# An fp32 encoder layer on one core: the down-projection as seven products of half blocks, and the weights' sums spread over four stages

## The chip, the cores and the metric

The kernel runs on one core of a Trainium2 chip. A core has TensorE for matmuls (PE in the profile, its weight loads PEld), VectorE (DVE), ScalarE (ACT), GpSimd (POOL) and SyncE (SP), which in this kernel issues every data transfer. The engines run side by side, each works off its own instructions in order, and semaphores join them. The metric is the device time of one execution in microseconds (us); less is better.

## The reference

One layer on two sequences of 512 tokens, width D = 1024, hidden width 2816, all in fp32. Cut to what matters:

```
mix = sigmoid(gla) * (oa @ w_o_a) + sigmoid(glb) * (ob @ w_o_b)   # "branches"
x = x + gt1 * (mix @ w_out)                                       # output projection
h2 = _rmsnorm(x, g_ffn) * (1 + sc2) + sh2
u = _dwconv(h2 @ w_up, conv_w, conv_b)                            # up-projection, 3-tap convolution over tokens
ua, ug = jnp.split(u, 2, axis=-1)
x = x + gt2 * ((jax.nn.silu(ug) * ua) @ w_down)                   # down-projection
```

Ahead of it stand the norm, the input projections and two kinds of attention (windowed, and over all keys with low-rank projections), which give oa and ob.

## The kernel before, in words

An fp32 operand is split into a high and a low part (`split_fast`: ACT casts, DVE subtracts; `split_pool`: both on POOL), and a product is three matmuls (`mm3`: high·high, high·low, low·high). A matmul takes 128 rows of the one operand against 512 columns of the other.

The stages follow each other on PE, with these starts in the profiled execution: input projections (0), attention with the gates' matmuls between (about 217 us), branches (600.6), output projection (693.4), up-projection (786), down-projection (1217.6).

**Up-projection.** It already is a scheme of seven products on half blocks, for each of 22 chunks of hidden columns: 84 matmuls a chunk instead of 96. It needs sums of the blocks of `w_up`. These are made ahead, during the attention, by the generator `weight_sums`: for each half of a chunk (128x4x256) it loads `wsum` (512 KB), does four POOL operations on it and stores it to `su_d` in DRAM. There are 44 halves, two buffers, and the attention's loop calls `next(wsum, None)` once a unit, three to a half. These instructions are pinned to program order (`keep_in_program_order`), and POOL also does the softmax's scaling (`p`, L539), for which PE's transposes (`ppt`, L545) wait.

**Branches.** `w_branch` loads a piece of w_o and splits it on POOL (`wo`, L70 and L73).

**Output projection.** `project_half(hf, order, between)` makes half the columns for all eight tiles of 128 tokens: 24 matmuls on `psx` a tile, a read-out on DVE, a store to `x1_d` (the trace writes `x_d`, since it leaves numbers out of names). `w_half(hf)` brings the weights in eight pieces through the ring `wraw` (seven buffers) and the ring `wt` (eight). So the eighth piece of `w_half(1)`, needed by the first tile of `project_half(1)`, is loaded only when the first piece has been split, and that waits for the last tile of `project_half(0)`.

**Down-projection.** `down_step(b, k)` brings and splits one block of gated values (`g_d`, stored by the up-projection) and two of `w_down`; for each sequence 22 blocks k, 4 row tiles, 2 column halves and 3 matmuls: 1056 matmuls on `psd`, both sequences one after the other on eight PSUM banks.

The order of the instructions on each engine is laid down when the kernel is built: a scheduler places them, within the rings of buffers and the pinned orders. SP too is in order, and an issue that waits for a semaphore holds all behind it.

Of the kernel before, what the change touches and what calls it, by code (L numbers as in the profile page):

```python
# [8 lines left out]
F32 = mybir.dt.float32  # L9
# [7 lines left out]
D = 1024  # L17
NB = 2
S = 512
TOK = NB * S  # L20
NT = S // 128
# [12 lines left out]
NP = FF // 128  # L34
EPS = 1e-6
# [4 lines left out]
def encoder_block(ctx, tc, x, c_t, w_ada0, b_col, w_ada, b_ada, cols, w_z, w_g, gains, tabs, sink,  # L40
# [11 lines left out]
    g_d = dram.tile([NB, NP, 128, S], F32, name="g_d")  # L52
# [403 lines left out]

    mp = ctx.enter_context(tc.tile_pool(name="mp", bufs=1))
# [5 lines left out]
    with ExitStack() as st:  # L463
# [37 lines left out]

        def weight_sums():

            pin = tc.keep_in_program_order
            halves = [(c, slice(256 * q, 256 * (q + 1))) for c in range(NP) for q in range(2)]
            ts = {}

            def load(n):  # L510
                if n < len(halves):
                    c, cs = halves[n]
                    ts[n] = gw.tile([128, 4, 256], F32, name="wsum", bufs=2)
                    pin(SY.dma_start(ts[n], w_up[c].rearrange("m q p n -> p (m q) n")[:, :, cs]))

            load(0)
            yield
            yield
            for n, (c, cs) in enumerate(halves):
                t = ts[n]  # L520
                load(n + 1)
                pin(G.tensor_add(t[:, 3], t[:, 2], t[:, 3]))
                pin(G.tensor_sub(t[:, 2], t[:, 0], t[:, 2]))
                yield
                pin(G.tensor_sub(t[:, 0], t[:, 3], t[:, 0]))
                pin(G.tensor_sub(t[:, 1], t[:, 1], t[:, 0]))
                yield
                pin(SY.dma_start(su_d[c, :, :, cs], t))
                yield
# [185 lines left out]
        wsum = weight_sums()  # L715
# [11 lines left out]
        for n in range(len(todo) + LAG + 2):  # L727
# [21 lines left out]
            next(wsum, None)  # L749
# [36 lines left out]
    with ExitStack() as s0:  # L786
# [33 lines left out]

        for f in range(0, KD, 2):
            wo = [w_branch(f), w_branch(f + 1)]
            for b in range(NB):
                for q in range(2):
                    branches(f + q, b, wo[q])
            if f == 4:
                ws = w_half(0)
# [7 lines left out]
    DOWN = ("st", "pt", "pt", "h", "h", "h", "h", "st")  # L835
    down = []

    def down_step(b, k):
        tag = DOWN[len(down) % 8]
        blk = hblk("wd", [128, 8 * S]) if tag == "h" else mblk("wd", tag, [128, 8 * S])  # L840
        w = blk[:, 0:4 * S].rearrange("p (a n) -> p a n", a=2)
        g = blk[:, 4 * S:6 * S].rearrange("p (a n) -> p a n", a=2)
        down.append((w, g))
        split_fast(g[:, 0], g[:, 1], wraw(g_d[b, k]))
        for hf in range(2):
            cs = slice(hf * 512, (hf + 1) * 512)
            (split_pool if hf else split_fast)(w[:, 0, cs], w[:, 1, cs], wraw(w_down[k * 128:(k + 1) * 128, cs]))
# [5 lines left out]
    with ExitStack() as s0:  # L853
# [94 lines left out]
        project_half(0, (0, 1), lambda b, i: None)  # L948
# [49 lines left out]
        def gated(c, b, ua, ug):  # L998
            A.activation(ug, ug, AF.Silu)
            V.tensor_mul(ua, ua, ug)  # L1000
            SY.dma_start(g_d[b, c], ua)
# [15 lines left out]
        def rest(c, w, px, val0, between=()):  # L1017
            between = iter(between)
            product(px, next(w), "t2", True)
            u2 = copied(px)  # L1020
            next(between, lambda: None)()
# [5 lines left out]
            next(between, lambda: None)()  # L1027
# [3 lines left out]
            V.tensor_add(u2, u2, py)  # L1031
            product(px, next(w), "t4", True)
            gated(c, 0, ua, conv1(c, 1, px))
            gated(c, 1, conv1(c, 0, u2), conv1(c, 1, p5))

        EARLY, HALVES = 4, 2
        wf = [list(weights_first(c)) for c in range(HALVES)]
# [10 lines left out]
        for c in range(HALVES, EARLY):  # L1048
            started.append(first(weights_first(c)))
            differences(c, c + 1)  # L1050

        for c in range(NP):
            if c < EARLY:
                rest(c, weights_rest(c), *started[c])
            else:
                w = weights_all(c)
                if c == NP - 1:
                    rest(c, w, *first(w), [lambda k=k: down_step(0, k) for k in (1, 2)])
                else:
                    rest(c, w, *first(w))  # L1060
                if c == NP - 2:
                    down_step(0, 0)


    with ExitStack() as s0:
        wk = s0.enter_context(tc.tile_pool(name="wke", bufs=2))
        LATE = 3
        for b in range(NB):
            gt = wk.tile([128, D], F32, name="gtf")
            SY.dma_start(gt, gt_d[1, b].partition_broadcast(128))  # L1070
            pss = [[bank("psd") for _ in range(2)] for _ in range(NT)]

            def products(i, k0, k1, halves=(0, 1)):
                for k in range(k0, k1):
                    w, g = down[b * NP + k]
                    for hf in halves:
                        cs = slice(hf * 512, (hf + 1) * 512)
                        sl = slice(i * 128, (i + 1) * 128)
                        mm3(pss[i][hf], g[:, 0, sl], g[:, 1, sl], w[:, 0, cs], w[:, 1, cs], k == 0, k == NP - 1)

            for k in range(NP):
                if len(down) == b * NP + k:
                    down_step(b, k)
# [85 lines left out]
```

## Time and profile before

| | |
|---|---|
| three runs | 1458.72, 1460.76 and 1462.15 us, median 1460.76 us |
| the profiled execution | 1463.69 us, its span in the trace 1461.9 us |
| granted TensorE clock, mean | 0.989 |
| PE busy | 95% of the span |
| DVE, ACT, POOL busy | 64%, 46%, 42% |

The span runs from the first to the last instruction of the trace. The shares are averages over stages with different limits. A granted clock of 1.00 is TensorE's full speed (2.4 GHz), 0.50 the lower level (1.2 GHz).

### The profile page before, as it was taken

To read this page: it belongs to the slowest core of one execution; us is meant where nothing else is said; L and a number is where in the kernel's file an instruction comes from. 1 tells how busy PE (TensorE), PEld (TensorE's weight loads), DVE (VectorE), ACT (ScalarE), POOL (GpSimd) and SP (SyncE) were. 2 spreads that over 40 slices of the span, in tenths; PEclk is the share of its full clock that TensorE was granted. 3 is DMA by queue.
4 is the path that set the end of the run, shared out by engine and by line. 5 is a ranking of instruction groups with operands and counts; after the bars stand their busy time and mean duration, and the time that the engine had idled before them with its cause. 6 is when DMAs were issued, how large, how long until landed. Compare 5 with 4: busy or idle time off the path is not lost.

```text
span 1461.9 us, 21179 instructions
## 1 busy us (share of the span) xinstructions
PE 1395.4 (95%) x7184; PEld 1155.7 (79%) x7184; DVE 941.7 (64%) x1885; ACT 679.5 (46%) x1385; POOL 609.0 (42%) x702
## 2 busy tenths in 40 slices
PE   5888997999999899999998999999999999999998
PEld 4777776888878787787887888888888887888887
DVE  4788774666668786564369776666666668347433
ACT  3475223666666566332136765555555554212210
POOL 3175023676677787455003232222222235444430
PEclk9999999999999999999999999999999999999999
DMA  8565764666666667855432344444434447646522
GB/s 320 195 209 178 239 234 159 196 227 202 227 198 220 208 212 250 286 174 177 143 115 80 108 130 130 125 127 123 130 123 127 132 122 250 205 140 222 185 80 72
DMA packets 162620, 255.19 MB, mean 175 GB/s; under 512 B 21192, under 2 KB 86984, under 8 KB 159440
## 3 DMA queue, kind: packets, MB, share of 16 engines
q1 hardware_dynamic: 162512, 253.84, 53.2%
q8 instruction: 57, 0.93, 0.3%
q14 instruction: 51, 0.42, 0.1%
HBM read 186.67 MB, written 67.13 MB: 174 GB/s over the span
## 4 chain that ended last, share of the span: by engine, by line
PE 78%; DVE 10%; DMA 5%; POOL 3%; ACT 2%; issue 2%; SPq 0%; ACTq 0%; POOLq 0%; DVEq 0%
PE px L980 15%; PE psg L495 9%; PE py L980 8%; PE psd L80 5%; PE psd L81 5%; PE psd L82 5%; PE pz L980 4%; PE ppt L545 3%; PE ppo L608 2%; PE psx L82 2%; PE psx L81 2%; PE psx L80 2%; PE psz L80 1%; PE psz L82 1%; PE psz L81 1%
## 5 line engine op out<-in xcount | busy, mean ns | idle before, releaser
L959 POOL TENSOR_TENSOR wt<-wraw,wt 128x512 fp32r<-128x512 f32 x88 | 119.4, 1363 | 395.4 <-ACT wt L958 362.9
L980 PE MATMUL px<-t,wt 128*128 128x512 f32 x792 | 190.0, 389 | 1.7 <-ACT tmp_cc L985 1.7
L980 PEld LDWEIGHTS px<-t,wt 128*128 128x128 f32 x792 | 148.5, 188 | 33.1 <-ACT tmp_cc L985 2.4
L495 PE MATMUL psg<-h_hi,wg 128*128 128x512 f32 x512 | 172.1, 401 | 0.0
L77 DVE TENSOR_TENSOR wd<-wraw,wd 128x512 fp32r<-128x512 f32 x88 | 96.3, 1133 | 90.8 <-ACT wd L76 90.8
L80 PE MATMUL psd<-wd 128*128 128x512 f32 x352 | 137.0, 389 | 0.1
L82 PE MATMUL psd<-wd 128*128 128x512 f32 x352 | 136.9, 389 | 0.0
L81 PE MATMUL psd<-wd 128*128 128x512 f32 x352 | 136.9, 389 | 0.0
L76 ACT CAST wd<-wraw 128x512 fp32r<-128x512 f32 x88 | 50.8, 619 | 151.5 <-issue 112.7
L958 ACT CAST wt<-wraw 128x512 fp32r<-128x512 f32 x154 | 93.9, 619 | 39.7 <-POOL wt L959 26.5
L495 PEld LDWEIGHTS psg<-h_hi,wg 128*128 128x128 f32 x512 | 97.0, 192 | 18.7 <-POOL wg L73 0.8
L539 POOL TENSOR_SCALAR p<-p,l 128x512 f32<-128x512 f32 (+2 forms) x128 | 78.3, 615 | 63.7 <-DVE l L538 45.9
L495 PE MATMUL psg<-h_lo,wg 128*128 128x512 f32 x256 | 102.7, 401 | 0.0
L537 ACT ACTIVATE p<-pps,nm 128x512 f32<-128x512 f32 (+2 forms) x128 | 78.1, 610 | 39.2 <-DVE nm L534 31.3
L992 DVE SCALAR_TENSOR_TENSOR tmp_u<-tmp_cc,cw,tmp_u 128x511 f32<-128x511 f32 x66 | 57.2, 867 | 41.5 <-ACT tmp_u L991 41.4
L70 POOL TENSOR_SCALAR wd<-wraw 128x512 fp32r<-128x512 f32 x44 | 33.6, 764 | 112.5 <-PE psd L82 84.9
L80 PEld LDWEIGHTS psd<-wd 128*128 128x128 f32 x352 | 66.1, 188 | 14.3 <-issue 0.5
L82 PEld LDWEIGHTS psd<-wd 128*128 128x128 f32 x352 | 66.1, 188 | 13.8
L81 PEld LDWEIGHTS psd<-wd 128*128 128x128 f32 x352 | 66.1, 188 | 13.5
L534 DVE TENSOR_REDUCE nm<-pps 128x1 f32<-128x512 f32 (+2 forms) x128 | 74.7, 584 | 3.2 <-PE pps L82 1.5
L545 PE MATMUL ppt<-ident,p 128*128 128x128 f32 x416 | 66.9, 274 | 8.2 <-POOL p L539 8.2
L73 POOL TENSOR_TENSOR wd<-wraw,wd 128x512 fp32r<-128x512 f32 x44 | 73.1, 1661 | 3.7
(256 smaller groups left out, 3425.7 us busy)
## 6 DMA issues: line engine op xcount, KB each, us to landing
w_ada<-in_w_ada_dram SPq DMA_DIRECT2D x24, 1024.0 KB, 5.5
wsum<-in_w_up_dram SPq DMA_DIRECT2D x44, 512.0 KB, 3.9
su_d<-wsum SPq DMA_DIRECT2D x44, 512.0 KB, 3.6
wraw<-su_d SPq DMA_DIRECT2D x88, 256.0 KB, 3.1
wraw<-in_w_down_dram SPq DMA_DIRECT2D x88, 256.0 KB, 3.2
wraw<-in_w_up_dram SPq DMA_DIRECT2D x66, 256.0 KB, 2.7
g_d<-tmp_u SPq DMA_DIRECT2D x44, 256.0 KB, 2.4
wraw<-g_d SPq DMA_DIRECT2D x44, 256.0 KB, 3.5
```

Of the source, the lines that this page charges most:

```text
L77: V.tensor_sub(lo, raw, hi.bitcast(F32))
L80: PE.matmul(ps, lhsT=lh, rhs=rh, start=first, stop=False)
L81: PE.matmul(ps, lhsT=lh, rhs=rl, start=False, stop=False)
L82: PE.matmul(ps, lhsT=ll, rhs=rh, start=False, stop=last)
L495: PE.matmul(ps, lhsT=ws[n][:, wl, k, :], rhs=hl[b][:, k, :], start=k == 0 and i == 0, stop=k == KD - 1 and i == 2)
L534: V.tensor_reduce(nm, ps[:, :n], op=ALU.max, axis=AX.X, negate=True)
L537: A.activation(p[:, :n], ps[:, :n], AF.Exp, bias=nm, accum_out=l)
L539: G.tensor_scalar(out=p[:, :plen], in0=p[:, :plen], scalar1=l, scalar2=1.0, op0=ALU.mult, op1=ALU.mult)
L545: PE.transpose(pt[:, j * 128:(j + 1) * 128], p[:, j * 128:(j + 1) * 128], ident)
L958: A.copy(w[:, 0], raw)
L959: lo_eng.tensor_sub(w[:, 1], raw, w[:, 0].bitcast(F32))
L980: PE.matmul(ps[:, sl], lhsT=w[:, wl, i], rhs=h[:, hl, sl], start=not add and i == 0 and n == 0, stop=i == 3 and n == 2, skip_group_check=add)
```

## The change

It has four parts.

1. **The sums of w_up in three places.** `weight_sums(tile, width, count)` now works through the chunks in the order `ORDER` (j, then j+11), of which the up-projection now also takes its chunks: 27 halves in the attention (a `next` at each of the first 62 units, then at every third), 6 halves in the branches (on `wt` tiles, three `next` after each branch), and the rest as 22 quarters of 128 columns in `project_half(0)` (on `cc` tiles, nine `next` after each tile).
2. **The down-projection as seven products.** With A the gated values (two sequences by two halves of the hidden width) and B the blocks of w_down, `PAIRS` names the seven products. Each has 11 steps j, 4 row tiles and 3 matmuls, 924 in all. `down_step()` brings one block of each operand (256 KB each), ACT casts both, DVE subtracts for the left one and DVE or POOL by turns for the right one. Four banks are one product's set, and there are two sets; later products add onto the banks of earlier ones.
3. **The sums for it in the up-projection.** `gated` writes to eight slots `gs`; `left_sums` (four POOL operations and four stores a pair of chunks) and `right_sums` (44 quarters of w_down: two loads, four POOL operations of 128x128, one store to `t_d`) are called from `between`, four times a chunk, right_sums twice a call in the chunks 5 to 20.
4. **Read-outs spread.** After each product four banks are read (one ACT copy or one DVE operation each), and the rest (a product with the gate, an addition of x, the store) goes to a list `later`, of which two entries are done a step, on POOL.

```diff
-        def weight_sums():
-            halves = [(c, slice(256 * q, 256 * (q + 1))) for c in range(NP) for q in range(2)]
+    quarters = [(c, 128 * q) for c in ORDER for q in range(4)]
+    def weight_sums(tile, width, count):
+        pin = tc.keep_in_program_order
+        def load(n):
+            if n < count and quarters:
+                c, c0 = quarters[0]
+                del quarters[:width // 128]
+                t, cs = tile(), slice(c0, c0 + width)
+                pin(SY.dma_start(t, w_up[c].rearrange("m q p n -> p (m q) n")[:, :, cs]))
+                return t, su_d[c, :, :, cs]
+        nxt, n = load(0), 0
+        yield
+        yield
+        while nxt:
+            n += 1
+            (t, dst), nxt = nxt, load(n)
+            pin(G.tensor_add(t[:, 3], t[:, 2], t[:, 3]))
+            pin(G.tensor_sub(t[:, 2], t[:, 0], t[:, 2]))
+            yield
+            pin(G.tensor_sub(t[:, 0], t[:, 3], t[:, 0]))
+            pin(G.tensor_sub(t[:, 1], t[:, 1], t[:, 0]))
+            yield
+            pin(SY.dma_start(dst, t))
+            yield
...
-            next(wsum, None)
+            if n < 62 or n % 3 == 2:
+                next(wsum, None)
...
-        project_half(0, (0, 1), lambda b, i: None)
+        wsum = weight_sums(lambda: tmp("cc").rearrange("p (m n) -> p m n", m=4), 128, 4 * NP)
+        def sums(b, i):
+            for _ in range(9):
+                next(wsum, None)
+        project_half(0, (0, 1), sums)
+        for _ in wsum:
+            pass
         ws = w_half(1)
...
+            def between():
+                next(lsum, None)
+                if n > EARLY and not last:
+                    for _ in range(2):
+                        next(rsum, None)
+                if last:
+                    down_step()
```

SP in the output projection before, from the second store of the first sequence on (`wraw_8304` is the eighth piece of `w_half(1)`):

```order
L885 DMA x1_d_65<-x1_0_8006 128x512
L954 DMA cw_8818<-in_conv_dram 128x176
L885 DMA x1_d_65<-x1_0_8006 128x512 x2
L901 DMA tmp_u0_8309<-gt_d_66 128x512
L885 DMA x1_d_65<-x1_0_8006 128x512
L885 DMA x1_d_65<-x1_1_8007 128x512 x3
L764 DMA wraw_8304<-in_w_out_dram 128x512
L764 DMA wraw_8820<-in_w_up_dram 128x512
```

SP at the same place now: how the quarters begin, and (behind the dots) what stands around the eighth piece, `wraw_8382`:

```order
L914 DMA x1_d_66<-x1_0_7930 128x512
L476 DMA tmp_cc_7967<-in_w_up_dram 128x4x128
L476 DMA tmp_cc_7969<-in_w_up_dram 128x4x128
L991 DMA cw_8896<-in_conv_dram 128x176
L491 DMA su_d_68<-tmp_cc_7967 512x1x128
L476 DMA tmp_cc_7976<-in_w_up_dram 128x4x128
L491 DMA su_d_68<-tmp_cc_7969 512x1x128
...
L491 DMA su_d_68<-tmp_cc_8190 512x1x128
L476 DMA tmp_cc_8236<-in_w_up_dram 128x4x128
L773 DMA wraw_8382<-in_w_out_dram 128x512
L773 DMA wraw_8898<-in_w_up_dram 128x512
```

The eighth piece stood behind stores of x1 alone; now it stands behind the stores of the first 15 quarters (`tmp_cc_8190` is the fifteenth), each with the load of the quarter after next behind it.

POOL in the last third of the attention before (scaling for the transposes, and the sums):

```order
L522 TENSOR_TENSOR wsum_5594<-wsum_5594 128x256
L523 TENSOR_TENSOR wsum_5594<-wsum_5594 128x256
L539 TENSOR_SCALAR p_5704<-p_5704,l_5705 128x384
L525 TENSOR_TENSOR wsum_5594<-wsum_5594 128x256
L526 TENSOR_TENSOR wsum_5594<-wsum_5594 128x256
L539 TENSOR_SCALAR p_5729<-p_5729,l_5730 128x384
L539 TENSOR_SCALAR p_5754<-p_5754,l_5755 128x256
L522 TENSOR_TENSOR wsum_5693<-wsum_5693 128x256
```

POOL in the same third now (L547 is the scaling):

```order
L547 TENSOR_SCALAR p_6068<-p_6068,l_6069 128x384
L547 TENSOR_SCALAR p_6094<-p_6094,l_6095 128x256
L547 TENSOR_SCALAR p_6131<-p_6131,l_6132 128x256
L547 TENSOR_SCALAR p_6154<-p_6154,l_6155 128x384
L547 TENSOR_SCALAR p_6177<-p_6177,l_6178 128x384
L485 TENSOR_TENSOR wsum_5949<-wsum_5949 128x256
L486 TENSOR_TENSOR wsum_5949<-wsum_5949 128x256
L547 TENSOR_SCALAR p_6205<-p_6205,l_6206 128x256
```

Between two halves of sums there now stand about nine scalings instead of three.

POOL in the middle of the up-projection before had the splits of one kind and nothing else:

```order
L959 TENSOR_TENSOR wt_9546<-wraw_9544,wt_9546 128x512
L959 TENSOR_TENSOR wt_9581<-wraw_9579,wt_9581 128x512
L959 TENSOR_TENSOR wt_9586<-wraw_9584,wt_9586 128x512
L959 TENSOR_TENSOR wt_9682<-wraw_9680,wt_9682 128x512
L959 TENSOR_TENSOR wt_9701<-wraw_9699,wt_9701 128x512
```

POOL there now (L1048 is `left_sums`, L1070 to L1073 `right_sums`, L996 the split that was L959):

```order
L996 TENSOR_TENSOR wt_10216<-wraw_10214,wt_10216 128x512
L1048 TENSOR_TENSOR gs_9193<-gs_9193 128x512 x4
L1070 TENSOR_TENSOR tmp_sf_9997<-tmp_sf_9997 128x128
L1071 TENSOR_TENSOR tmp_sf_9997<-tmp_sf_9997 128x128
L1072 TENSOR_TENSOR tmp_sf_9997<-tmp_sf_9997 128x128
L1073 TENSOR_TENSOR tmp_sf_9997<-tmp_sf_9997 128x128
...
L1070 TENSOR_TENSOR tmp_sf_10125<-tmp_sf_10125 128x128
L996 TENSOR_TENSOR wt_10328<-wraw_10326,wt_10328 128x512
```

The splits for the products now queue behind the sums on POOL. (At the dots stands a further quarter of the same form.)

## Rows read from the trace of the kernel before

**Rows 1.** The page, busy time of each engine in the whole span.

```profile
PE 1395.4 (95%) x7184; PEld 1155.7 (79%) x7184; DVE 941.7 (64%) x1885; ACT 679.5 (46%) x1385; POOL 609.0 (42%) x702
```

**Rows 2.** Windows: stretch, its length, busy time and count of each engine, clock, DMA.

```profile
900.00:1000.00 100.00, 100.00 (x443) 82.83 (x442) 63.22 (x84) 55.03 (x90) 26.15 (x20) 1.00 0.43 126
1300.00:1400.00 100.00, 100.00 (x443) 82.84 (x442) 54.88 (x54) 21.58 (x38) 46.36 (x38) 1.00 0.56 186
```

**Rows 3.** The tile psd on PE: ns min/median/max, first and last start.

```profile
L80 PE MATMUL psd<-wd x352: 389/389/468, 1217.6 to 1456.7; 128*128 128x512 f32 x176
```

**Rows 4.** Waits by pair, 250 to 620 us: total, times, longest.

```profile
POOL wsum L522 <- DMA wsum<-in_w_up_dram: 30.0, 14, 4.8
PE ppt L545 <- POOL p L539: 8.2, 5, 3.4
```

**Rows 5.** Timeline of POOL and of PE, 493 to 499 us.

```profile
495.73 0.72 POOL L522 TENSOR_TENSOR wsum<-wsum 128x256 f32<-128x256 f32 x1 [4.84 <-DMA wsum<-in_w_up_dram]
497.23 1.60 POOL L539 TENSOR_SCALAR p<-p,l 128x256 f32<-128x256 f32 x3
497.76 0.44 PE L545 MATMUL ppt<-ident,p 128*128 128x128 f32 x2 [3.36 <-POOL p L539]
```

**Rows 6.** Windows around the stalls of the attention.

```profile
480.00:520.00 40.00, 35.28 (x193) 29.51 (x191) 29.04 (x88) 23.19 (x61) 30.49 (x45) 0.96 0.70 222
580.00:600.00 20.00, 16.45 (x69) 13.26 (x67) 8.29 (x11) 3.92 (x9) 14.02 (x17) 0.91 0.70 225
```

**Rows 7.** Waits of PE by pair, 600 to 800 us.

```profile
PE psy L82 <- POOL wo L73: 2.8, 3, 1.5
PE psy L80 <- POOL wo L70: 1.5, 2, 0.8
```

**Rows 8.** The tile psx on PE, then timelines of DVE and SP, 693 to 740 us.

```profile
L80 PE MATMUL psx<-wt,m_hi x128: 389/389/500, 693.4 to 785.4; 128*128 128x512 f32 x128
705.08 0.69 DVE L884 TENSOR_TENSOR x<-tmp_u,x 128x512 f32<-128x512 f32 x1
705.80 0.33 SPq L885 DMA_DIRECT2D x_d<-x  x1
733.78 0.33 SPq L764 DMA_DIRECT2D wraw<-in_w_out_dram  x1
739.09 0.68 DVE L77 TENSOR_TENSOR wt<-wraw,wt 128x512 fp32r<-128x512 f32 x1
```

**Rows 9.** SP's waits 430 to 610 us, then its timeline at 486 us.

```profile
SPq L528 <- POOL wsum L526: 33.2, 13, 4.4
486.28 0.52 SPq L528 DMA_DIRECT2D su_d<-wsum  x1
```

**Rows 10.** Tiles wsum and wt on POOL; landing of wsum (512 KB); issues of wraw.

```profile
L522 POOL TENSOR_TENSOR wsum<-wsum x44: 722/734/1124, 251.6 to 591.4; 128x256 f32<-128x256 f32 x44
L959 POOL TENSOR_TENSOR wt<-wraw,wt x88: 1263/1296/2850, 786.6 to 1199.0; 128x512 fp32r<-128x512 f32 x88
DMA to landing us min/median/max: 3.2/3.7/8.2
wraw<-su_d SPq DMA_DIRECT2D x88, 256.0 KB, 3.1
wraw<-in_w_up_dram SPq DMA_DIRECT2D x66, 256.0 KB, 2.7
```

**Rows 11.** PE after its idle time at 219 us, and the window behind it.

```profile
223.94 1.11 PE L159 MATMUL psa<-ident,br 128*128 128x128 f32 x4 [5.00 <-DVE br L156]
224.00:230.00 6.00, 6.00 (x19) 4.91 (x20) 2.06 (x13) 0.00 (x0) 0.85 (x3) 0.59 0.33 115
```

**Rows 12.** Groups by form, 1218 to 1462 us: busy, mean ns, idle before.

```profile
L77 DVE TENSOR_TENSOR wd<-wraw,wd 128x512 fp32r<-128x512 f32 x77 | 86.6, 1163 | 90.2 <-ACT wd L76 90.2
L73 POOL TENSOR_TENSOR wd<-wraw,wd 128x512 fp32r<-128x512 f32 x39 | 65.4, 1677 | 3.3
L76 ACT CAST wd<-wraw 128x512 fp32r<-128x512 f32 x75 | 43.1, 619 | 148.1 <-issue 112.7 <-PE psd L82 21.1 <-DMA wraw<-in_w_down_dram 12.3
```

More of the change, by code (lines that the diff above doesn't have):

```diff
@@ L1055, in encoder_block @@
             else:
                 w = weights_all(c)
[L1057 to L1062, printed above, removed]
+                rest(c, w, *first(w), between)
+            if c >= HP:
+                for _ in lsum:
+                    pass
+                lsum = left_sums(c - HP)
+        for _ in lsum:
+            pass
@@ L1065, in encoder_block @@
+        for _ in rsum:
+            pass
     with ExitStack() as s0:
[L1066 to L1067 removed]
+        wk = s0.enter_context(tc.tile_pool(name="wke", bufs=1))
+        AHEAD, LATE = 4, 3
+        gts = []
         for b in range(NB):
[L1069 removed]
+            gt = wk.tile([128, D], F32, name=f"gtf{b}")
             SY.dma_start(gt, gt_d[1, b].partition_broadcast(128))
[L1071 to L1083, printed above, removed]
[L1084 to L1101 removed]
@@ new lines, in encoder_block, with x1_tile, store @@
+            gts.append(gt)
+        sets = [[bank("psd") for _ in range(NT)] for _ in range(2)]
+        q1 = mblk("q1", "st", [128, NT, S], F32)
+        vw = mblk("vw", "st", [128, 2, NT, S], F32)
+        later = []
+        def x1_tile(b, i, n):
+            xt = wk.tile([128, 512], F32, name="xe", bufs=6)
+            t = b * NT + i
+            SY.dma_start(xt, x1_d[t * 128:(t + 1) * 128, n * 512:(n + 1) * 512])
+            return xt
+        def store(b, i, n, src):
+            t = b * NT + i
+            SY.dma_start(out[t * 128:(t + 1) * 128, n * 512:(n + 1) * 512], src)
@@ new lines, in c21, with tile_product @@
+        def c21(i, ps, xt):
+            y = ytile()
+            for h in range(2):
+                cs = slice(h * 256, (h + 1) * 256)
+                V.tensor_mul(y[:, cs], ps[:, cs], gts[1][:, cs])
+                V.tensor_add(y[:, cs], y[:, cs], q1[:, i, cs])
+                t = NT + i
+                SY.dma_start(out[t * 128:(t + 1) * 128, cs], y[:, cs])
+        def tile_product(ps, i, n, first, last, add):
+            sl = slice(i * 128, (i + 1) * 128)
+            g, w, _ = down[n]
+            for m, (gi, wi) in enumerate(((0, 0), (0, 1), (1, 0))):
+                PE.matmul(ps, lhsT=g[:, gi, sl], rhs=w[:, wi], start=first and not add and m == 0,
+                          stop=last and m == 2, skip_group_check=add)
```

191 lines of the change are left out of this document (128 added, 63 removed).

## The prediction

> **What bounds the kernel now.** I read the page's shares first: PE is busy 95% of the span, no other engine above 64% [rows 1]. A share says nothing of the stages, so I looked at windows next. In the up- and the down-projection PE is busy 100 us of 100 at full clock, with 443 matmuls in each stretch, so one costs 100 / 443 = 0.226 us [rows 2]. (The 389 ns that the tile's view gives for one are pipelined and overlap; the pace is what counts.) The 1056 matmuls of psd stand between 1217.6 and about 1457.2 us: 0.227 each, with no gap [rows 3]. There, time falls only with the number of matmuls, and any engine that comes late adds its lateness in full.
>
> Then the waits of PE. In the attention, transposes wait 8.2 us in 5 times for POOL's scaling, while POOL waits 30.0 us for loads of wsum [rows 4]. The timeline shows one such stall whole: POOL sits 4.84 us for a load of wsum, does two sums of the half, comes to the scaling at 497.23, and PE, which needs that, starts after 3.36 us idle [rows 5]. After the stalls the granted clock is below 1.00: 0.96 over 40 us and 0.91 over 20 us [rows 6], which is 40 x 0.04 + 20 x 0.09 = 3.4 us lost. The branches lose 4.3 us to POOL's splits of wo in two groups of waits [rows 7]. The output projection has no PE idle time of note, but little slack, as shown below.
>
> **The change, part by part.** All terms are against the profiled execution's 1463.7 us, which is 2.9 above the median of the runs; I take this off at the end.
>
> *Seven products.* 1056 - 924 = 132 matmuls less, at 0.2265 us: **-29.9**. They are of the same shape, so this holds as long as PE stays the bound.
>
> *Sums in the attention.* The last third of the units keeps a third of the sums; their loads are issued some six scalings ahead of their use, so the waits of rows 4 should go, and the lost clock with them: 8.2 + 3.4 = 11.6. The sums in the first 62 units stay, and a few small stalls may appear elsewhere, for which I take off 1.1: **-10.5** (bounds: -11.6, all of it; -5, if the two long stalls of some 3.4 us come back elsewhere).
>
> *Sums in the branches.* 6 halves x 4 operations x 0.74 us = 18 us more of POOL in the first seven branches, each 24 matmuls = 5.4 us of PE. The wait there is already for POOL, but wo is split a pair of pieces ahead, and the 6 halves spread: **+0.5** (-1 to +3, where the upper end lets a third of the 18 us minus the idle time of POOL come through).
>
> *Quarters in the output projection.* This is the term that I take as the main loss. Call T0 = 693.4, the first psx [rows 8]. The order of SP shows two facts. The first quarter's load stands behind the first store of x1, and that was issued at 705.80, after DVE's 705.08 operation [rows 8]: T0 + 12.4. And the eighth piece of w_out's second half stands behind the store of the fifteenth quarter. SP holds everything behind an issue that waits: before, stores of sums made SP wait 33.2 us for POOL, and one issue took 0.52 us [rows 9]. Between, each load of a quarter is issued behind the store of the second last one. So two quarters are in flight, and a cycle of two is: store issued (0.5), load issued and landed, POOL's four operations, the next store.
>  - POOL: a 128x256 sum takes 0.73, a 128x512 one 1.30 [rows 10], so 128x128 by the same line 0.45, with the gap about 0.5: 2.0 a quarter (an estimate from these rows).
>  - Landing: 256 KB takes 2.7 to 3.1, the 512 KB of wsum 3.7 (median), which is cut into short rows like the quarter [rows 10]. I take 3.1, because it has the same size under a like load; both ends are kept.
>  - Cycle: 0.6 + 3.1 + 0.1 + 2.0 = 5.8 us for two quarters. The first is done at T0 + 12.8 + 3.1 + 0.1 + 2.0 = T0 + 18.0, the fifteenth seven cycles later, at T0 + 58.6.
>  - Then 1.1 us for store, load and issue, 3.1 to land, 0.62 to cast and 0.68 to subtract: the piece is there at T0 + 64.1.
>  - PE needs it after eight tiles and seven pieces: 8 x 24 x 0.227 + 21 x 0.227 = T0 + 48.4. Before, the load was issued at 733.78 and the split ended at 739.77 = T0 + 46.4 [rows 8]: a slack of 2.0.
>
> So PE sits idle about 16 us. With 2.7 to land it is 13, with 3.7 it is 20, and if loads came without any delay POOL alone (14 x 2.0) would make it 3. After an idle time of 5.00 us the next 6 us ran at 0.59 [rows 11], a loss of 2.5; I add that, and 0.5 for stores of x1 that stand behind the last quarters: **+19** (+4 to +25).
>
> The Trainium skill's page "DMA: Bandwidth & Descriptors" (section "Anatomy of one DMA") puts a transfer at about 2.0 us fixed plus its bytes over 436 GB/s. By that, an estimate of 2.6 us for 256 KB, the idle time would be 12 us, and the sum 4 us lower than mine; the trace's medians for this size are above it.
>
> *Up-projection.* A pair of chunks is 168 matmuls = 37.9 us of PE. POOL gets per pair 8 splits at 1.30 [rows 10], 4 sums of 128x512 at the same, and 32 of 128x128 at 0.50 to 0.54: 10.4 + 5.2 + 16 to 17.3 = 32 to 33 us, against 10.4 before. That is 84 to 87% of the pair; it fits, but only just. A chunk's weights are split about a chunk ahead, which covers what comes in bursts. Transfers grow from 126 GB/s to an estimated 190, the down-projection's present 186 [rows 2]: hidden. **+2** (0 to +10).
>
> *Read-outs and steps of the down-projection.* A step is 12 matmuls = 2.72 us; ACT has two casts at 0.62 [rows 12], DVE one or two subtractions at 0.69 to 1.16 [rows 8, 12], 512 KB to bring is 193 GB/s. Four of the six borders of products reuse banks; the first bank must be read within 9 matmuls = 2.0 us, and four read-outs on DVE behind a running subtraction just make it. **+1.5** (0 to +4).
>
> Sum: -29.9 - 10.5 + 0.5 + 19 + 2 + 1.5 = -17.4, so 1446.3 for an execution like the profiled one and **1443** for a median run.
>
> **The rivals.**
>
> *The sums keep pace in the output projection.* If the eighth piece came in time, only the 2 or 3 us of small terms would stay of the +19: -29.9 - 10.5 + 0.5 + 2 + 1.5 = -36.4, so 1427 and at the median **1424**. It asks for a quarter each 1.8 us, as (48.4 - 5.5 - 18.0) / 14; POOL's own 2.0 speaks against it. For it: if the trace's SP could pass a waiting store, nothing in the rest of the stage needs the sums early; but rows 9 show the waits.
>
> *The attention gains nothing*, because the remaining sums stall POOL at other units: 10.5 higher, **1454**. Against it: with fewer sums in the stretch that stalled, there are fewer loads to wait for.
>
> *POOL becomes the bound of the up-projection, slower than before.* The splits of the same shape take 1.30 in the median beside a DVE that is 63% busy [rows 2, 10], but 1.68 (mean) in the down-projection, where DVE's subtractions stretched too, to 1.16 from 0.68 in the output projection [rows 8, 12]. The mean stretch there is 1.68 / 1.30 = 1.29, the worst of the sums in the attention 1124 / 734 = 1.53 [rows 10]. POOL is the bound from 37.9 us a pair on, a stretch of 1.17. At 1.29 a pair costs 42 us: 4 us over, 5.5 pairs, 22 less about 10 of lead, +12, and 1455. It ends slower than before from +20.7 on, which is 43.5 us a pair or a stretch of 1.34. At 1.4, about the middle of the two rows, a pair costs 45.5: 7.6 x 5.5 - 10 = +32, **1475**. Against it: in the up-projection itself, with DVE at 63%, the median split is not stretched at all.
>
> The Trainium skill's "GPSIMD Engine Reference" (section "Specifications") says that GpSimd shares its SBUF interfaces with VectorE and contends with DVE instructions that have two SBUF inputs. By that rule this rival would be the likely one, since most of DVE's operations here have two; the stretched rows agree with it, the median of the up-projection does not.
>
> **How the numbers follow.** Forecast 0.58, sums that keep pace 0.18, no gain in the attention 0.08, POOL as the bound 0.12 (the half of it slower than before), other 0.04. The likeliest one's own range, from the ends of its terms that don't all come together, is 1434 to 1453. To leave out no more than 2 in 10 the range must reach the first rival, the second and the lower half of the third: 1422 to 1463. A difference under 0.2% (2.9 us) cannot be told from none here. Slower takes the upper half of the third rival and most of "other", 0.09; within 0.2% a slice of the second and third, 0.05; faster the rest, 0.86.
>
> **What would show it.** psd has 924 matmuls, and first to last start is about 211 us; the transposes' waits for the scaling after 430 us are gone and the clock is 1.00 there. In the output projection PE waits some 16 us, at about 48 us after the first psx, for the last split of wt; SP issues that piece some 60 us after the first psx, directly behind a store of su_d; the clock is 0.50 after it. POOL is busy some 85% of the up-projection's second half and PE has no wait for it above 1 us. The prediction is wrong if the quarters take less than 2 us each, if the up-projection's chunks take more than 19.0 us, or if the wait in the output projection is there but hides something that I have counted once more.

## The result, and the profile after

The changed kernel takes 1546.95 us (median of 4 runs, 1541.44 to 1554.83) against 1460.53: a ratio of 1.0596, 95% interval 1.0547 to 1.0645. It is slower by 86 us. The prediction said 1443, faster.

The profiled execution took 1545.7 us, 82.0 more than the one before, so it can be laid stage by stage beside it. The lengths come from the first starts of psg, psy, psx, px and psd in the views by tile (down: first to last start). The change does not touch what stands ahead of the attention: over the thirteen traces of this document that stretch ends between 212.1 and 217.3 us, so its -3.9 is no effect of the change.

| us | before | after | difference | forecast |
|---|---|---|---|---|
| up to the attention | 216.6 | 212.7 | -3.9 | 0 |
| attention | 384.0 | 367.6 | -16.4 | -10.5 |
| branches | 92.8 | 103.3 | +10.5 | +0.5 |
| output projection | 93.2 | 117.3 | +24.1 | +19 |
| up-projection | 431.0 | 489.6 | +58.6 | +2 |
| down-projection | 239.6 | 248.6 | +9.0 | -28.4 |

The page of the changed kernel, busy time of each engine (it answers to [rows 1]); then the tiles on PE, with first and last start (to [rows 3, 8]):

```profile
PE 1400.2 (91%) x7052; PEld 1151.4 (75%) x7052; DVE 986.5 (64%) x1917; ACT 720.6 (47%) x1455; POOL 781.3 (51%) x944
```

```profile
L86 PE MATMUL psy<-o,wo x128: 389/389/637, 580.3 to 683.0; 128*128 128x512 f32 x128
L86 PE MATMUL psx<-wt,m_hi x128: 387/389/792, 683.6 to 799.7; 128*128 128x512 f32 x128
L1017 PE MATMUL px<-h,wt x288: 278/389/582, 800.9 to 1273.9; 128*128 128x512 f32 x120, 128*128 128x256 f32 x24
L1224 PE MATMUL psd<-wt,gl x924: 387/389/796, 1290.5 to 1539.1; 128*128 128x512 f32 x185
```

132 matmuls are gone, as planned, and yet the last stage is longer. The waits of PE over the whole span (total, times, longest) say where the time is:

```profile
PE px L1017 <- ACT tmp_cc L1022: 24.5, 5, 5.1
PE psx L86 <- ACT wt L82: 17.8, 1, 17.8
PE psd L1224 <- DVE ye L1205: 13.9, 2, 7.6
...
PE py L1017 <- ACT tmp_cc L1022: 12.8, 5, 3.2
PE psd L1224 <- ACT q L1186: 8.5, 2, 7.1
...
PE psd L1224 <- DVE vw L1195: 6.6, 1, 6.6
PE psy L86 <- POOL wo L76: 6.5, 4, 3.1
```

There are five pairs of stalls in the up-projection (37.3 us), one stall in the output projection (17.8) and stalls at four borders of products in the down-projection (29.0). Most of the rest is clock: windows of the up-projection and of the first border (columns as in [rows 2]; the clock stands ahead of the last two).

```profile
950.00:1000.00 50.00, 42.05 (x163) 33.68 (x162) 27.35 (x31) 19.71 (x33) 33.28 (x43) 0.86 0.60 186
1050.00:1100.00 50.00, 43.12 (x172) 34.49 (x170) 29.18 (x34) 20.99 (x35) 34.82 (x46) 0.90 0.63 198
1290.50:1350.00 59.50, 51.04 (x214) 41.28 (x213) 28.90 (x37) 26.20 (x47) 19.20 (x13) 0.91 0.73 238
430.00:580.00 150.00, 148.45 (x827) 125.72 (x825) 118.44 (x358) 95.43 (x251) 76.06 (x116) 1.00 0.41 136
```

The last row is the attention's second part: the clock is back at 1.00 and PE is busy 148.45 of 150 us, so the gain that was forecast there is real.

**The output projection went by the chain that was forecast.** SP around the eighth piece of `w_half(1)`, and PE behind it:

```profile
738.76 0.52 SPq L491 DMA_DIRECT2D su_d<-tmp_cc  x1
...
744.57 0.52 SPq L491 DMA_DIRECT2D su_d<-tmp_cc  x1
745.13 0.63 SPq L476 DMA_DIRECT2D tmp_cc<-in_w_up_dram  x1
745.80 0.55 SPq L773 DMA_DIRECT2D wraw<-in_w_out_dram  x1
```

```profile
749.90 0.79 PE L86 MATMUL psx<-wt,m_hi 128*128 128x512 f32 x1 [17.82 <-ACT wt L82]
```

The last two of the fifteen quarters take 744.57 - 738.76 = 5.81 us (5.8 was worked out). Over all of them the cycle is longer: the first store is issued at 699.78 and the fifteenth at 744.57, which is 6.4 us for two. The first store came 1.8 us sooner after the first psx than worked out (16.2 against 18.0), which takes back part of it. So the piece is issued 62.2 us after the first psx (59.7 by the prediction's sum), and PE waits 17.8 us (16).

**The up-projection: the same thing, once for each of five pairs of chunks.** SP, then ACT and PE, in one such stretch:

```profile
1001.77 0.56 SPq L1075 DMA_DIRECT2D t_d<-tmp_sf  x1
1002.38 1.30 SPq L1062 DMA_DIRECT2D tmp_sf<-in_w_down_dram  x2
1005.85 0.56 SPq L1075 DMA_DIRECT2D t_d<-tmp_sf  x1
1006.45 1.30 SPq L1062 DMA_DIRECT2D tmp_sf<-in_w_down_dram  x2
1007.79 0.60 SPq L773 DMA_DIRECT2D wraw<-in_w_up_dram  x1
...
1014.10 1.98 SPq L773 DMA_DIRECT2D wraw<-su_d  x4
1016.16 1.37 SPq L773 DMA_DIRECT2D wraw<-in_w_up_dram  x3
```

```profile
1010.99 0.62 ACT L995 CAST wt<-wraw 128x512 fp32r<-128x512 f32 x1 [8.83 <-POOL tmp_sf L1072]
...
1012.23 0.56 ACT L1022 COPY tmp_cc<-px 128x512 f32<-128x512 f32 x1
1018.37 1.24 ACT L995 CAST wt<-wraw 128x512 fp32r<-128x512 f32 x2 [5.58 <-DMA wraw<-su_d]
```

```profile
1012.84 4.61 PE L1017 MATMUL px<-t,wt 128*128 128x512 f32 x12 [4.87 <-ACT tmp_cc L1022]
1020.15 4.51 PE L1017 MATMUL py<-e,wt 128*128 128x512 f32 x12 [2.70 <-ACT tmp_cc L1022]
```

The reader is to see three queues, one behind the other. SP brings only one piece of the weights between 987 and 1014 us, since the stores of eight quarters stand around it, 2.7 to 7.0 us apart (983.12 to 1011.51, a mean of 4.1); then seven pieces in 4 us. ACT sits 8.83 us ahead of a weight's cast at 1010.99. The view names POOL there, but what the cast reads is the piece that SP issued at 1007.79, 3.2 us earlier, and 3.2 us is the median landing of such pieces in this stage. The copy that frees PE's bank (L1022) stands behind that cast. The view of PE names the copy; the cause is two queues further back. The pair takes some 50 us (PE starts again at 1012.84, and after the same stall one pair later at 1062.37) in place of 37.9.

### The profile page after: what moved, and what is told of

It reads as the page before. It is cut to its first block, busy times and chain, and to the rows that moved or that the text cites. A ratio compares the mean times of both kernels' runs of the same rounds, so it can differ in the third digit from the quotient of the medians.

```text
span 1543.9 us, 21610 instructions
## 1 busy us (share of the span) xinstructions
PE 1400.2 (91%) x7052; PEld 1151.4 (75%) x7052; DVE 986.5 (64%) x1917; ACT 720.6 (47%) x1455; POOL 781.3 (51%) x944
## 4 chain that ended last, share of the span: by engine, by line
PE 50%; POOL 15%; DMA 11%; issue 11%; DVE 9%; ACT 2%; SPq 2%; POOLq 0%; DVEq 0%; ACTq 0%
PE px L1017 10%; PE psg L532 10%; PE py L1017 6%; PE ppt L553 3%; DMA tmp_cc<-in_w_up_dram 2%; PE psd L1224 2%; PE pz L1017 2%; POOL gs L1048 2%; PE ppo L616 2%; POOL wt L875 2%; DMA wraw<-a_d 2%; DMA wraw<-su_d 1%; DMA tmp_sf<-in_w_down_dram 1%; PE psz L86 1%; POOL wt L996 1%
## 5 line engine op out<-in xcount | busy, mean ns | idle before, releaser
L1224 PE MATMUL psd<-wt,gl 128*128 128x512 f32 x924 | 220.0, 401 | 29.0 <-DVE ye L1205 13.9
L1224 PEld LDWEIGHTS psd<-wt,gl 128*128 128x128 f32 x924 | 179.2, 195 | 69.7 <-ACT wt L874 15.0
L996 POOL TENSOR_TENSOR wt<-wraw,wt 128x512 fp32r<-128x512 f32 x88 | 123.7, 1411 | 200.3 <-ACT wt L995 200.2
L995 ACT CAST wt<-wraw 128x512 fp32r<-128x512 f32 x154 | 94.0, 618 | 119.4 <-DMA wraw<-in_w_up_dram 35.6
L83 DVE TENSOR_TENSOR gl<-wraw,gl 128x512 fp32r<-128x512 f32 x77 | 62.8, 818 | 113.8 <-ACT gl L82 113.4
L547 POOL TENSOR_SCALAR p<-p,l 128x512 f32<-128x512 f32 (+2 forms) x128 | 78.4, 615 | 104.9 <-DVE l L546 54.1
L875 POOL TENSOR_TENSOR wt<-wraw,wt 128x512 fp32r<-128x512 f32 x38 | 51.3, 1349 | 135.4 <-ACT wt L874 134.8
L1029 DVE SCALAR_TENSOR_TENSOR tmp_u<-tmp_cc,cw,tmp_u 128x511 f32<-128x511 f32 x66 | 70.4, 1067 | 61.4 <-ACT tmp_u L1028 61.3
L996 DVE TENSOR_TENSOR wt<-wraw,wt 128x512 fp32r<-128x512 f32 x66 | 69.5, 1072 | 32.4 <-ACT wt L995 32.2
L1017 PE MATMUL py<-e,wt 128*128 128x512 f32 x264 | 72.3, 428 | 12.8 <-ACT tmp_cc L1022 12.8
L1048 POOL TENSOR_TENSOR gs<-gs 128x512 f32<-128x512 f32 x44 | 73.4, 1678 | 3.8 <-DVE gs L1039 2.4
L1017 PEld LDWEIGHTS py<-e,wt 128*128 128x128 f32 x264 | 54.6, 209 | 27.5 <-ACT tmp_cc L1022 15.5
L1017 PE MATMUL px<-h,wt 128*128 128x512 f32 (+1 forms) x288 | 67.3, 378 | 2.7 <-POOL wt L996 2.4
L1031 DVE SCALAR_TENSOR_TENSOR tmp_u<-tmp_cc,cw,tmp_u 128x511 f32<-128x511 f32 x66 | 67.5, 1023 | 1.4
```

What stands on the lines that cost most here:

```text
L547: G.tensor_scalar(out=p[:, :plen], in0=p[:, :plen], scalar1=l, scalar2=1.0, op0=ALU.mult, op1=ALU.mult)
L875: (G if n % 2 else V).tensor_sub(w[:, 1], raw, w[:, 0].bitcast(F32))
L995: A.copy(w[:, 0], raw)
L996: lo_eng.tensor_sub(w[:, 1], raw, w[:, 0].bitcast(F32))
L1017: PE.matmul(ps[:, sl], lhsT=w[:, wl, i], rhs=h[:, hl, sl], start=not add and i == 0 and n == 0, stop=i == 3 and n == 2, skip_group_check=add)
L1029: V.scalar_tensor_tensor(out=u[:, 1:S], in0=src[:, 0:S - 1], scalar=cw[:, cc, 0:1], in1=u[:, 1:S], op0=ALU.mult, op1=ALU.add)
```

## The experiments

Lengths of stages in us, from the profiled executions as in the table above; the ratio is to the runs of before on the same chip.

| | median us | ratio (95%) | attention | branches | output | up | down |
|---|---|---|---|---|---|---|---|
| the change | 1546.95 | 1.0596 (1.0547 to 1.0645) | 367.6 | 103.3 | 117.3 | 489.6 | 248.6 |
| e1_wraw8 | 1546.49 | 1.0558 (1.0535 to 1.0581) | 369.6 | 102.1 | 120.2 | 485.2 | 250.2 |
| e2_gstore | 1562.0 | 1.0670 (1.0644 to 1.0695) | 372.4 | 102.2 | 126.2 | 493.5 | 248.9 |
| e3_ahead2 | 1552.45 | 1.0602 (1.0578 to 1.0625) | 370.5 | 103.6 | 115.1 | 486.3 | 256.1 |
| e4_sums_att | 1533.72 | 1.0475 (1.0452 to 1.0498) | 385.4 | 92.6 | 93.1 | 492.4 | 252.1 |
| e5_pin | 1524.95 | 1.0413 (1.0368 to 1.0458) | 372.8 | 102.2 | 119.4 | 493.4 | 219.6 |
| e6_norsum | 1493.4 | 1.0214 (1.0183 to 1.0245) | 370.4 | 103.1 | 118.9 | 429.6 | 248.8 |
| e7_vsums | 1537.44 | 1.0522 (1.0496 to 1.0548) | 369.0 | 102.6 | 116.2 | 473.2 | 251.1 |
| e8_all | 1483.55 | 1.0149 (1.0124 to 1.0175) | 382.8 | 93.9 | 93.2 | 471.6 | 215.1 |
| e9_thin | 1453.65 | 0.9955 (0.9928 to 0.9981) | 380.4 | 91.6 | 93.1 | 445.0 | 217.0 |
| e10_twoops | 1538.39 | 1.0537 (1.0510 to 1.0563) | 367.5 | 103.6 | 115.2 | 478.3 | 254.8 |
| e11_thin12 | 1450.98 | 0.9927 (0.9911 to 0.9943) | 385.1 | 92.9 | 98.5 | 437.9 | 215.7 |

**An eighth buffer for wraw.** To tell whether the piece's place behind the stores is the cause in the output projection:

```diff
-        r = wp.tile([128, 512], F32, name="wraw", bufs=7)
+        r = wp.tile([128, 512], F32, name="wraw", bufs=8)
...
-            xt = wk.tile([128, 512], F32, name="xe", bufs=6)
+            xt = wk.tile([128, 512], F32, name="xe", bufs=5)
```

(The second pair of lines makes room; `xe` belongs to the down-projection.)

> The ring wraw gets an eighth buffer (xe one less, to make room), so that the eighth piece of w_half(1) is issued ahead of the quarters' stores. Theory (SP's queue: the piece stood behind stores that wait for POOL): the idle time of 17.8 us in the output projection and the 5 or 6 us of half clock after it go, 1546.9 to about 1524 us; the up- and the down-projection keep their stalls. Rival (the second half is late because PE, ACT and POOL share memory with the quarters' sums, or because the stores of x1 wait too): no more than 5 us faster, 1542 to 1547.

It took 1546.49. The wait for the piece is gone, and waits of a like size stand behind it (waits of PE in this kernel; 24.6 of the 27.0 us lie in this stage):

```profile
PE pst L895 <- DVE x L921: 27.0, 4, 14.4
```

PE's transposes now wait for tiles of x1, whose buffer `u1` comes free with the stores of x1, and these stand on SP behind the last quarters: the first tile of the second half, which DVE had made by 734.9 us, is stored at 763.31. The stage even grew by 3 us. So the theory "it is this piece" is too narrow: everything that SP issues in this stage stands behind the sums, and a second late thing takes the place of the first. The sum of the prediction had given it 0.5 us, because it is hidden while the first wait stands.

**Stores issued by POOL.** All three kinds of stores of sums:

```diff
-                pin(SY.dma_start(dst, t))
+                pin(G.dma_start(dst, t))
...
-                SY.dma_start(a_d[LEFT[nm], j], o)
+                G.dma_start(a_d[LEFT[nm], j], o)
```

> All stores of sums (quarters, left and right sums, halves) are issued by POOL in place of SP, so that SP never waits for POOL's sums; POOL's work grows by the issues. Theory (SP's queue): the idle time of 37 us and the half clock after it in the up-projection mostly go, and the 17.8 us in the output projection too; 1546.9 to 1470 to 1485 us. Rival (POOL's own throughput beside DVE is the bound of a pair of chunks): the up-projection stays at about 490 us or grows, only the output projection gains; 1525 us or more.

It took 1562.0; the up-projection stayed at 493.5, as the rival said, so the theory that SP alone is the cause falls. The rival's other half, a gain in the output projection, did not come either (126.2 against 117.3). Waits of SP from 812 to 1306 us, and the group of the issues on POOL (busy, mean ns, idle before):

```profile
SPq L773 <- POOL wt L996: 246.8, 74, 12.7
```

```profile
L1075 POOL DMA_DIRECT2D t_d<-tmp_sf x44 | 32.4, 736 | 10.8 <-POOL tmp_sf L1073 8.9 <-issue 1.9
```

SP now waits for POOL by another way: the buffers of wraw come free with POOL's splits, and these stand on POOL behind the same run of quarters, each 0.74 us longer by its issue. In the output projection SP's loads of quarters wait for their own buffers (45.3 us in 16 waits, until the stores have landed), the piece stands behind those, and PE waits 30.0 us for it.

**Two steps ahead in place of four.** In the down-projection, `AHEAD, LATE = 4, 3` becomes `AHEAD, LATE = 2, 3`.

> In the down-projection two steps are brought ahead of the products in place of four. Theory (the read-outs at a border stand on ACT and DVE behind the splits of the steps ahead, whose loads come late): each of the four waits of about 7 us shrinks by two steps of some 2.5 us, 16 to 20 us less with the half clock that follows; 1546.9 to about 1528 us. Rival (the read-outs themselves, or loads that are late whatever the order): the waits stay or get longer, 1545 us or more.

1552.45: no gain. But this edit does not tell the two theories apart. In the traces of both kernels ACT has 20 casts of left blocks ahead of the first read-out (9 more than the product has steps), and DVE has 32, 43, 54 and 65 subtractions for left blocks ahead of the next ones: the scheduler, not AHEAD, sets how far the splits run in front.

**The sums of w_up back in the attention.**

```diff
-        wsum = weight_sums(lambda: gw.tile([128, 4, 256], F32, name="wsum", bufs=2), 256, 27)
+        wsum = weight_sums(lambda: gw.tile([128, 4, 256], F32, name="wsum", bufs=2), 256, 44)
...
-            if n < 62 or n % 3 == 2:
-                next(wsum, None)
+            next(wsum, None)
```

> The first part of the change undone: all 44 halves of the sums of w_up are made in the attention again, at every unit; nothing in the branches and the output projection. Theory (each stage pays for what it was given by itself): the attention gives back its 16 us, the branches gain 10 and the output projection 24 us; 1546.9 to about 1529 us, and up- and down-projection stay as they are (490 and 249 us). Rival (the spread was worth it, the loss in the output projection would appear elsewhere, for example as a later start of the up-projection's weights): 1540 us or more.

1533.72. The stages do what the theory says: attention +17.8, branches -10.7, output projection -24.2 against the change, all within 2 us of their lengths before. The other two stages are 2.8 and 3.5 longer, which is not explained; the medians differ by 13 us in place of 18. But this kernel ran on another chip, where the kernel before took 1464.68 too, 4 us more; by the two ratios, each to before on its own chip, the gain is 1.2% or 17.7 us. The first part of the change, alone, costs some 17 to 18 us.

**Splits in program order in the down-projection.** The question of e3 again, with an edit that reaches it:

```diff
-        split_fast(g[:, 0], g[:, 1], wraw(a_d[LEFT[name], j]))
-        A.copy(w[:, 0], raw)
-        (G if n % 2 else V).tensor_sub(w[:, 1], raw, w[:, 0].bitcast(F32))
+        pin = tc.keep_in_program_order if n >= 4 else lambda ins: ins
+        graw = wraw(a_d[LEFT[name], j])
+        pin(A.copy(g[:, 0], graw))
+        pin(V.tensor_sub(g[:, 1], graw, g[:, 0].bitcast(F32)))
+        pin(A.copy(w[:, 0], raw))
+        pin((G if n % 2 else V).tensor_sub(w[:, 1], raw, w[:, 0].bitcast(F32)))
```

> The splits of the down-projection's steps from the fifth on are kept in the order in which the program gives them, so that a product's read-outs stand on ACT and DVE behind 14 steps' splits in place of 20 (the first border), 25 in place of 32 and so on: 3 steps ahead in place of 9 or 10. Theory (the waits of about 7 us at four borders come from read-outs queued behind splits of later steps, whose loads have not landed): the four waits shrink to 1 to 3 us each and the down-projection from 249 to about 220 us; 1546.9 to about 1520 us. Rival (the splits are late in themselves, by their loads, and PE would wait for the operands in place of the banks): 249 us and 1546 us stay, with waits for wt or gl.

1524.95, the stage 219.6. The tile psd on PE in this kernel, and what PE still waits for:

```profile
L1227 PE MATMUL psd<-wt,gl x924: 387/389/795, 1300.5 to 1520.1; 128*128 128x512 f32 x185
its engine sat idle before it (us, times) until:
  ACT wt L877: 3.1, 2
  POOL wt L878: 1.7, 2
  DVE ye L1208: 0.8, 1
```

29.0 us of waits became 5.6, and ACT has 14 casts of left blocks ahead of its first read-out in place of 20. In the changed kernel's trace the cause can be read too: ACT's first read-out starts at 1327.00, 6.5 us after PE had stopped (its last matmul of the product ends at 1320.55), and between stand six casts, of which three wait for a load.

```profile
1323.06 0.62 ACT L82 CAST gl<-wraw 128x512 fp32r<-128x512 f32 x1 [1.73 <-DMA wraw<-a_d]
...
1325.95 0.62 ACT L82 CAST gl<-wraw 128x512 fp32r<-128x512 f32 x1 [0.95 <-DMA wraw<-a_d]
1326.48 0.61 ACT L874 CAST wt<-wraw 128x512 fp32r<-128x512 f32 x1
1327.00 0.58 ACT L1186 COPY q<-psd 128x512 f32<-128x512 f32 x1
```

**No sums of w_down.** `rsum = iter(())`, and the products read plain blocks of w_down.

> The sums of w_down are left out (the products read plain blocks of w_down in their place). Theory (the eight quarters a pair of chunks, in a row on POOL and on SP ahead of the next weights, make the five long stalls of the up-projection): the up-projection falls from 490 to 435 us or less, with no half clock; 1546.9 to about 1490 us. Rival (the left sums, the eight slots gs or the order of the chunks are the cause): 475 us or more remain.

1493.4; the up-projection is 429.6, as before the change. A window of 250 us in it:

```profile
950.00:1200.00 250.00, 250.00 (x1104) 207.08 (x1103) 182.79 (x211) 136.94 (x224) 108.63 (x77) 1.00 0.46 145
```

PE is busy 250 of 250 at full clock. So the right sums make the whole loss of the stage, and the left sums, the slots gs and the new order of chunks cost nothing by themselves. It does not tell whether it is the sums' transfers, their operations or their run.

**The sums of w_down on DVE.** The four operations with V in place of G.

> The four operations of each quarter of w_down's sums run on DVE in place of POOL; all transfers stay where they are. Theory (POOL's long run of quarters holds both its own splits and, through the stores, SP): the up-projection falls from 490 to 440 to 450 us, 1546.9 to about 1500 us, although DVE's share grows from some 58% to 75% of the stage. Rival (the chain store, load, landing on SP is long enough by itself, or DVE becomes the bound): 480 us or more remain.

1537.44; the stage is 473.2, between the two. Together with the edits of e4 and e5 it is the next kernel.

> The three edits together: sums of w_up all in the attention, w_down's sums on DVE, the down-projection's splits kept in program order. If each theory holds: attention 384, branches 92.6, output projection 93, up-projection 440, down-projection 220, about 1445 us, faster than before by 15. If the rivals hold, 1500 us or more.

1483.55: every stage but the up-projection is within 5 us of what was expected, and that is 471.6, as in e7. Waits of DVE in it, 900 to 1180 us:

```profile
DVE tmp_sf L1072 <- DMA tmp_sf<-in_w_down_dram: 19.4, 15, 3.3
```

The quarters now stand on DVE and wait there for their loads, and what PE's banks need stands behind them. In one stall DVE waits 2.61 us for a quarter's load (until 1036.56), does an addition (L1086) at 1038.78 and not before, ACT's next step waits 3.79 us for that, and PE starts again at 1040.83 after a wait of 5.16 us for ACT's copy. This queue too is in order.

**Half the run of quarters.** On e4 and e5 together, `right_sums(tag, n0, n1)` is called for 8 quarters in `project_half(0)` (two `next` a tile) and for 36 in the up-projection:

```diff
                 if n > EARLY and not last:
-                    for _ in range(2):
+                    for _ in range(2 if n < 8 else 1):
                         next(rsum, None)
```

> On the kernel with all sums of w_up in the attention and the down-projection's splits in program order: the 44 quarters of w_down's sums run on POOL and SP as in the change, but one a tile in the first half of the output projection (8) and then 2 a chunk in place of 4 (4 in the first three chunks that have any). Theory (a pair of chunks costs the run of quarters, which holds POOL's splits and SP, plus the refill of the weights behind it, one after the other): with half the run a pair fits its 37.9 us, the up-projection falls to 432 to 445 us; about 1440 to 1455 us in all, faster than before. Rival (POOL and DVE stretch each other, or the transfers are too many, whatever the spacing): the up-projection stays above 465 us; 1475 us or more.

1453.65, 0.9955 of before: faster by less than half a per cent, in an interval (0.9928 to 0.9981) that leaves out 1; its ten runs spread from 1445 to 1462 us, and the profiled one (1446.29) is among the shortest. Its waits in the up-projection that are left (9.3 us of px and py for copies, in 3 times) suggested the three chunks that still have four quarters.

**Two of four operations left out.** On the changed kernel, the third and fourth operation of each quarter are gone, so T2 and T4 are not made; transfers stay.

> The changed kernel with two of the four operations of each quarter of w_down's sums left out; transfers and order stay. Theory (the length of POOL's run of quarters counts): a run of eight quarters is 8 to 9 us shorter, so each of the five stalls of some 11 to 13 us shrinks to 3 to 5; the up-projection falls from 490 to 450 us and the whole to about 1507 us. Rival (SP's chain of store, load and landing sets the pace, not POOL): 480 us and 1537 us or more remain.

1538.39; the stage 478.3, 11 us less, not 40. POOL's waits, 900 to 1180 us:

```profile
POOL tmp_sf L1070 <- DMA tmp_sf<-in_w_down_dram: 19.4, 15, 2.5
```

With half its work POOL waits for the quarters' loads (7.3 us in the changed kernel, same stretch), and from its second store to its eighth SP's run of quarters is still 20.7 us long, against 24.1 (983.37 to 1004.08 here, 987.44 to 1011.51 there). That is the rival's side, nearly: POOL's operations on the quarters are not the main part of the loss, as half of them is worth 11 of 58 us. What is left of a run is SP's chain of store, two loads and landing, but also POOL's left sums (6.84 us in a row at 984.68 in the changed kernel) and splits that stand between the quarters; no run parts these.

**12 quarters early, two a chunk later.** `right_sums("cc", 0, 12)` with three `next` a tile, and one `next` a call in every chunk from the sixth on.

> The previous kernel (one quarter a tile in the output projection and two a chunk later) with the three chunks of four quarters thinned too: 12 quarters in the first half of the output projection (1.5 a tile of 5.4 us, slower than the 2.9 to 3.5 us that a quarter's chain takes) and two a chunk from the sixth chunk on. Theory (only a run of eight quarters in front of the weights stalls the up-projection): its last waits of some 9 us in the first such chunks go, the stage falls from 445 to about 432 us and the whole to about 1440 us, 0.986 of before; no wait in the output projection. Rival (the first chunks stall for another reason, or 12 quarters hold the eighth piece): 1450 us or more.

1450.98, 0.9927 of before. The up-projection fell from 445.0 to 437.9, and PE's waits for copies there are 4.6 us, none over 0.9. The output projection paid 5 us for the 12 quarters (3.1 us of it a wait of psx for the split of wt), so the rival had a share as well, and its time (1450 or more) is the one that came. The up-projection keeps 32 of the 44 quarters here.

## Why the prediction was wrong, point by point

- **Fewer matmuls, -29.9: right.** The kernels whose borders are mended take 215 to 220 us in the down-projection against 239.6, with PE's remaining waits in it; 239.6 - 29.9 would be 209.7.
- **Attention, -10.5: right, somewhat small** (-16.4). The waits for the scaling are gone (none of ppt is left from 430 to 580 us) and the clock is 1.00. In the one pair of traces it went beyond my bound of -11.6, which held only one pair of waits. Over all traces the effect is nearer to the bound: the eight kernels with the change's attention take 367.5 to 372.8 us there (mean 370.0), the five with all sums in it 380.4 to 385.1 (mean 383.5). What gave the 2 us or so beyond the bound was not tested.
- **Output projection, +19: right** (+24.1), by the chain worked out: the quarters' stores hold the eighth piece, and PE waits 17.8 us. The cycle was 6.4 us in the mean, not 5.8, and an earlier start hid part of that. The ends of the landing (13 and 20 us of idle time) changed it in the seven cycles alone; with the first quarter's and the piece's own landing they would be 12 and 21. By the Trainium skill's page "DMA: Bandwidth & Descriptors" (section "Anatomy of one DMA"), whose figures are for transfers that GpSimd issues while these go out by SP, the cycle would have been an estimated 0.5 us shorter; the quarters' loads landed in 3.3 us (median of 22), on the side of the row's 3.1 that I took.
- **Branches, +0.5: mis-sized** (+10.5; e4 gives 10.7 back). I let POOL's 18 us pass for hidden and did not price SP. PE's waits grew from 5.1 to 10.4 us, and the clock fell to 0.90 to 0.95 over the last 64 us of the stage, an estimated 5 us more. Of the longer waits, that at 603 us is for a split of wo behind twelve operations on halves in a row on POOL, and that at 633 for a piece of wo that SP could issue only behind a half's store, which waited for POOL. The longest (3.1 us, at 657.94) stands behind POOL's splits of w_out.

```profile
601.86 0.73 POOL L489 TENSOR_TENSOR wsum<-wsum 128x256 f32<-128x256 f32 x1
602.55 1.20 POOL L76 TENSOR_SCALAR wo<-wo_raw 128x512 fp32r<-128x512 f32 x2
...
625.56 0.52 SPq L491 DMA_DIRECT2D su_d<-wsum  x1
626.82 1.92 SPq L813 DMA_DIRECT2D wo_raw<-in_w_o_dram  x3
632.48 0.62 POOL L76 TENSOR_SCALAR wo<-wo_raw 128x512 fp32r<-128x512 f32 x1 [4.99 <-DMA wo_raw<-in_w_o_dram]
```

- **Up-projection, +2: the step that failed, with 57 us.** "It fits, but only just" compared POOL's work with a pair's time, and "A chunk's weights are split about a chunk ahead, which covers what comes in bursts" was taken from the kernel before. But the weights of a pair stand, on SP and on POOL both, behind a run of eight quarters, 4.1 us apart in the mean; run and refill come one after the other, and their sum, some 50 us, exceeds the 37.9. Without the run the stage takes 429.6 us (e6), with two quarters a chunk in place of four 437.9 (e11). I had worked out this very chain for the output projection and did not apply it here, though the order of SP shows the same rows. My third rival had the right stage and a wrong mechanism: POOL's work did stretch, to about 38 us a pair (8 splits at 1.41, 4 left sums at 1.68, 8 quarters at 2.5 with gaps), but 38 us of work alone would not make a pair 50 us long, and POOL was busy only 34.8 of 50 us [window 1050 to 1100 above]. That it contends with DVE agrees with the Trainium skill's "GPSIMD Engine Reference" (section "Specifications"): the convolution's first operation on DVE took 1077 ns (mean) here and 850 before. But the stretch by itself did not make the loss: in e11 the convolution's first operation takes 1021 ns and a split on POOL 1.43 us, much as here (1077 and 1.41), and the stage is only 7 us longer than before. As e11 also halves the quarters that a pair gets, it does not tell a shorter run from less work for each pair; for the run speak POOL's idle time and e10.
- **Borders of the down-projection, +1.5: the second step that failed, with 37 us.** "The first bank must be read within 9 matmuls ... and four read-outs on DVE behind a running subtraction just make it" assumed that one subtraction stands ahead of a read-out. There were the splits of 9 or 10 steps on DVE, and on ACT, which reads out at the first border, their casts, some still waiting for loads. I had not looked at the order of ACT and DVE at the borders. With that order mended (e5) the waits fell from 29.0 to 5.6 us.
- **The sums.** These two steps are 94 of the 99 us between the forecast of -17.4 and the 82.0 measured. In the sum of my first rival the 2 or 3 us that it says would stay are not counted. e11, with both steps mended and the sums of w_up back in the attention, comes to 0.9927 of before; the forecast of 1443 would have been 0.988.

What stays open: how a quarter's time in the up-projection divides exactly between SP's chain and POOL (e10 bounds only POOL's operations on the quarters, and the left sums and splits between them were not parted), the last 7 us of the stage in e11, and how the loss in the branches divides between POOL's order and SP's.

## What to carry to other kernels

Work that an engine has time for is not free if its transfers share an in-order queue with the bound's operands: price a run by its length in that queue (store, load, landing, operations), ask what stands behind it, and do so in every stage that gets such a run. When one late item is freed, look for the next one behind the same queue: here moving a buffer, the stores or the operations gave at most 18 us of the stage's 58, and spacing the run out gave all but 7. A read-out at a product's border is as late as the slowest split that the order puts in front of it, so look at that order on the reading engines, not only at the bank's deadline.

## What the runs showed of the hardware

An issue of a transfer by POOL took 0.74 us of POOL (mean of 44), beside the four operations of 128x128 of about 0.46 us each when undisturbed. The same operation on DVE had a mean of 0.29 us for the first of the four and 0.70 for the second (e8, 42 of each); POOL's splits and sums ran beside both, and why the second is hit so much more was not tested. The stretch on DVE went with where an operation reads: the convolution's first operation on DVE, with both large inputs in SBUF (tmp_cc and tmp_u), went from 850 to 1077 ns in the mean when POOL got the sums; the same operation with one of them in a bank that PE writes (px) took 749 before and 748 after.
